# State space stage: outer products through PSUM, recursion by pairs and fours, pads in three pools

## The chip, the cores and the metric
The kernel runs on one core of a Trainium2 chip. The metric is the device time of one launch in microseconds (us), as the median of several runs. Times inside an execution come from one profiled run, in us from the start of its span. The engines are PE (TensorE, the matmuls; PEld are its weight loads), DVE (VectorE), ACT (ScalarE), POOL (GpSimd) and SP, which here only issues DMAs.

## The reference
Two networks in a row on 256 tokens of width 1024, batch 1, all in float32. The first block is a state space (S5) mixer, a squared-ReLU MLP and a gate; the second is two layers of a mixer with four branches and a gated MLP, with shift, scale and gate vectors made from a conditioning vector by `w_ada`. The change lies in the mixer of the first block:

```
ab  = exp(lam * dt)                       # (64 groups, 64 states), complex
bb  = (ab - 1) / lam * b                  # input matrices, 16 channels a group
bu  = einsum('blgh,gph->blgp', u, bb)     # complex
xs[t] = ab * xs[t-1] + bu[t]              # over the 256 tokens
y   = Re(xs @ c) + d * u
out = gated linear unit of gelu(y)
...
mod = silu(c_2) @ w_ada + b_ada           # 6 vectors for each later layer ("ada")
```

## The kernel before, in words
The kernel is built with a scheduler, which lays the instructions of each engine in one fixed order; each engine then runs its own list and waits on semaphores.

The mixer cuts the 256 tokens into 32 chunks of 8. It has five parts.

1. *Parameters.* `s5_params` makes the powers of `ab` (`pr`, `pi` for exponents in a chunk, `pr2`, `pi2` for the output side) by small DVE operations of 128x32.
2. *The b products.* For each of eight group sets `b_outer` (L597 to L602) multiplies `bb` by powers: DVE makes two products (L597, L600), POOL two others (`ta`, L598, `tb`, L601), DVE combines them (L599, L602) into `pt`. PE transposes `pt` (L655), ACT copies it (`pmt`, L656), PE multiplies `u` with it (L660), ACT copies (`ss`, L662), PE transposes again (L666), ACT writes `zb` (L670): the state that each chunk adds.
3. *The scan.* 30 steps over the chunks (L677 to L680), four DVE operations of 128x64 each: two products, two sums. Every step needs the one before. Then four halves are swapped (L686 to L688) so that `zb` can be the weights of the last product.
4. *The c products.* Sixteen calls of `c_outer` make `ca`, the output matrices times powers: a DVE product (L780), a POOL product (L781) and a sum, on DVE in eight calls and on POOL in eight (L782). From `ca` PE makes the kernel inside a chunk (`kt`, L708), ACT copies it (L716), 32 small DMAs lay it out as `mt` (L720, 27 of them in SP's queue, 5 in POOL's).
5. *The outputs.* PE multiplies `u` by `mt` (L739) and, into the same PSUM tiles, `ca` by `zb` (L751); then come transposes (L762), a gelu and the split into a high and a low part (`y`), and the gated linear unit ("glu"), the first of the long matmuls (L363 to L365, three for each product).

Between these, `ada_next` puts steps of the ada product on PE as filling: a step reads a tile `wa` of 512 KB by SP (L916) into one of three buffers and multiplies it in eight matmuls of 128x256 (L918). The steps that are not done in the mixer are done between the matmuls of glu (seven pairs, the second step of a pair split into four pieces between glu's matmuls) and in the MLP (eight single ones).

DVE and the SBUF side of POOL are shared by parts 2 to 4; the order of SP's queue is that of the code (ada reads, then `mt`, then the weights of the next stage).

Of the kernel before, what the change touches and what calls it, by code (L numbers as in the profile page):

```python
# [9 lines left out]
F32 = mybir.dt.float32  # L10
# [3 lines left out]
ALU = mybir.AluOpType  # L14
# [3 lines left out]
P = 128  # L18
# [260 lines left out]
class Net:  # L279
# [19 lines left out]
    def _t(self, pool, tag, shape, dt, s):  # L299
        tag = tag + self.ln  # L300
        pool = self.late.get(tag, pool)
        return pool.tile(list(shape), dt, tag=tag, bufs=BUFS[tag], name=self.nm(s))

    def k4(self, shape, dt=F32, s="k4"):
        return self._t(self.p4, "k4", shape, dt, s)
# [190 lines left out]
    def s5_params(self):  # L496
# [80 lines left out]
                f, g = slice(64 * half, 64 * half + 64), slice(32 * half, 32 * half + 32)  # L577
                self.S.copy(self.bb3[r, g, 0::2], bb[f, ri].unsqueeze(2).to_broadcast([64, 32, 2, 16]))

        arr, aii = (self.q6.tile([P, 2, 32], F32, name=s) for s in ("arr", "aii"))  # L580
        for r in range(2):
            V.tensor_copy(arr[:, r, :], pr[:, :, 0])
        V.tensor_scalar(aii[:, 0, :], pi[:, :, 0], -1.0, None, op0=ALU.mult)
        V.tensor_copy(aii[:, 1, :], pi[:, :, 0])
        self.arr, self.aii = arr, aii

    def b_outer(self, dst, g0, xr, xi):

        V, G = self.V, self.G
        sh = [P, 4, 8, 16]  # L590
        pr = self.pr[:, g0 : g0 + 4, :].unsqueeze(3).to_broadcast(sh)
# [8 lines left out]
        V.tensor_tensor(dst[:, :, 1], xi, pr, op=ALU.mult)  # L600
        G.tensor_tensor(tb, xr, pi, op=ALU.mult)  # L601
        V.tensor_tensor(dst[:, :, 1], dst[:, :, 1], tb, op=ALU.add)  # L602

    def s5(self):
        V, G, S, T, nc = self.V, self.G, self.S, self.T, self.nc
# [36 lines left out]
        V.memset(zb[:, :, :, 0:1], 0.0)  # L642
        bre, bim = self.bb[:, 0], self.bb[:, 1]
        for jp in range(4):
            ss_sb = self.k4([P, 2, 2, 2, 64], F32, "ss")
            for jj in range(2):
                pt = self.q4.tile([P, 4, 2, 8, 16], F32, tag="pt", name=self.nm("pt"))
                self.b_outer(pt, (jp * 2 + jj) * 4, bre, bim)
                self.ada_next(2)
                pmt = self.k4([P, 4, 2, P], F32, "pmt")  # L650
                for g2 in range(2):
                    ps = self.pm([P, 4, P])
                    for i in range(4):
                        g4, ri = g2 * 2 + i // 2, i % 2
# [13 lines left out]
            for jj in range(2):  # L668
                g0 = (jp * 2 + jj) * 4
                S.copy(zb[:, :, g0 : g0 + 4, 1:32], ps[:, jj, :, :, 0:31])  # L670


        for s in range(1, 31):
            prev, nxt = zb[:, :, :, s], zb[:, :, :, s + 1]
            t1 = self.sm([P, 2, 32])
            t2 = self.sm([P, 2, 32])
            V.tensor_tensor(t1, prev, self.arr, op=ALU.mult)  # L677
            V.tensor_tensor(t2, zb[:, ::-1, :, s], self.aii, op=ALU.mult)
            V.tensor_tensor(t1, t1, nxt, op=ALU.add)
            V.tensor_tensor(nxt, t1, t2, op=ALU.add)  # L680
            if s in (23, 30):

                c = slice(0, 24) if s == 23 else slice(24, 32)
                t = self.bb.rearrange("p a (b e) c -> p (a b) (e c)", e=2)
                cp = V.tensor_copy if s == 23 else S.copy
                cp(t[64:128, :, c], zb[0:64, 1, :, c])  # L686
                V.tensor_copy(zb[0:64, 1, :, c], zb[64:128, 0, :, c])
                cp(zb[64:128, 0, :, c], t[64:128, :, c])  # L688
# [12 lines left out]
        for half in range(2):  # L701
# [898 lines left out]
    def run(self):  # L1600
        tc, nc = self.tc, self.nc
        V, S, G = self.V, self.S, self.G
        with ExitStack() as st:
# [8 lines left out]
            self.psm = pool("psm", 3, space=PSUM)  # L1612
            self.psx = pool("psx", space=PSUM)
# [4 lines left out]
            self.late = {}  # L1618
# [4 lines left out]
            with ExitStack() as s5s:  # L1623
# [145 lines left out]
```

## Time and profile before

| | |
|---|---|
| median of 3 runs | 1995.99 us (1995.98 to 1996.63) |
| the profiled execution's own time | 1997.63 us |
| its span | 1995.9 us |
| PE busy | 1906.2 us (96%) |
| DVE busy | 1548.6 us (78%) |
| ACT busy | 927.4 us (46%) |
| POOL busy | 130.9 us (7%) |
| chain that ended last | PE 84%, DVE 11%, issue 2%, DMA 2%, ACT 1% |

The span is the time from the first to the last instruction; the time of the execution is a little longer. In the page's 40 slices of 49.9 us each, PE is busy in tenths `3869999999...`: it is not full in the first three slices, where the mixer stands, and full from the fourth on. DVE has `9974577699...`: full in the first two.

### The profile page before, as it was taken

What the parts mean: (1) busy time and instruction counts of PE and PEld (TensorE: products, weight loads), DVE (VectorE), ACT (ScalarE), POOL (GpSimd) and SP (SyncE); (2) the same over time, 40 slices, a digit from 0 to 9 for tenths busy, and PEclk for the clock granted to TensorE, in tenths of its full rate; (3) what the DMA queues carried; (4) which work ended last, traced back from release to release, by engine and by line L of the source; (5) the groups of instructions that cost most, each with busy time, mean ns of one, the idle gap of its engine ahead of it and who ended that gap; (6) DMA issues with size and microseconds to landing.
All of it is one profiled execution on the core that took longest, in us unless ns stands there. A gap on an engine that the chain in (4) does not pass through costs nothing.

```text
span 1995.9 us, 35545 instructions
## 1 busy us (share of the span) xinstructions
PE 1906.2 (96%) x13842; PEld 1692.7 (85%) x13842; DVE 1548.6 (78%) x3133; ACT 927.4 (46%) x1583; POOL 130.9 (7%) x138
## 2 busy tenths in 40 slices
PE   3869999999999999999999999999999999999998
PEld 1457899998789998789998777787998789999997
DVE  9974577699987789998778576675689997776665
ACT  2443445455654555664553212212555664544443
POOL 6720000000000011000000000000100000010000
PEclk8989999999999999999999999999999999999998
DMA  5657665554345564236555455454455235555663
GB/s 176 187 187 244 224 199 183 180 183 156 106 125 169 182 191 156 88 106 189 181 187 157 126 163 164 152 165 124 141 178 157 74 108 170 180 180 169 183 187 107
DMA packets 103192, 323.45 MB, mean 162 GB/s; under 512 B 16416, under 2 KB 18608, under 8 KB 102640
## 3 DMA queue, kind: packets, MB, share of 16 engines
q1 hardware_dynamic: 102256, 319.53, 51.3%
q8 instruction: 109, 1.79, 0.4%
q0 software_dynamic: 336, 1.44, 0.2%
q14 instruction: 59, 0.48, 0.1%
q10 hardware_dynamic: 432, 0.21, 0.0%
HBM read 317.47 MB, written 1.05 MB: 160 GB/s over the span
## 4 chain that ended last, share of the span: by engine, by line
PE 84%; DVE 11%; issue 2%; DMA 2%; ACT 1%; SPq 0%; DVEq 0%; ACTq 0%
PE pm L363 21%; PE pm L364 21%; PE pm L365 21%; PE pm L1029 2%; PE pm L1031 2%; PE pm L1030 2%; DVE wl L332 2%; PE px L1351 1%; DVE cy L1060 1%; PE px L1300 1%; PE pm L372 1%; PE pm L373 1%; PE px L918 1%; PE pm L374 1%; PE px L1333 1%
## 5 line engine op out<-in xcount | busy, mean ns | idle before, releaser
L331 ACT CAST wh<-ws 128x1024 fp32r<-128x1024 f32 (+3 forms) x556 | 533.1, 961 | 723.7 <-PE pm L364 410.2
L332 DVE TENSOR_TENSOR wl<-ws,wh 128x1024 fp32r<-128x1024 f32 (+3 forms) x556 | 616.5, 1116 | 267.0 <-ACT wh L331 264.5
L363 PE MATMUL pm<-h,wh 128*128 128x256 f32 (+1 forms) x928 | 301.1, 324 | 0.0
L365 PE MATMUL pm<-h,wl 128*128 128x256 f32 (+1 forms) x928 | 299.5, 323 | 0.0
L364 PE MATMUL pm<-h,wh 128*128 128x256 f32 (+1 forms) x928 | 298.9, 322 | 0.0
L363 PE MATMUL pm<-m,wh 128*128 128x256 f32 (+1 forms) x704 | 213.7, 304 | 0.0
L364 PE MATMUL pm<-m,wh 128*128 128x256 f32 (+1 forms) x704 | 213.2, 303 | 0.0
L365 PE MATMUL pm<-m,wl 128*128 128x256 f32 (+1 forms) x704 | 212.6, 302 | 0.0
L363 PEld LDWEIGHTS pm<-h,wh 128*128 128x128 f32 x928 | 176.1, 190 | 20.7 <-ACT wh L331 4.6
L364 PEld LDWEIGHTS pm<-h,wh 128*128 128x128 f32 x928 | 176.2, 190 | 15.9 <-issue 0.8
L365 PEld LDWEIGHTS pm<-h,wl 128*128 128x128 f32 x928 | 175.7, 189 | 14.9
L363 PE MATMUL pm<-hx,wh 128*128 128x256 f32 x640 | 184.0, 288 | 0.0
L364 PE MATMUL pm<-hx,wh 128*128 128x256 f32 x640 | 180.6, 282 | 0.0
L365 PE MATMUL pm<-hx,wl 128*128 128x256 f32 x640 | 180.2, 281 | 0.0
L1060 DVE SCALAR_TENSOR_TENSOR cy<-up,vecs,cy 128x256 f32<-128x256 f32 x360 | 162.6, 485 | 1.4
L363 PEld LDWEIGHTS pm<-m,wh 128*128 128x128 f32 x704 | 134.1, 191 | 8.5 <-ACT wh L331 1.7
L364 PEld LDWEIGHTS pm<-m,wh 128*128 128x128 f32 x704 | 134.2, 191 | 6.6 <-issue 1.7
L952 DVE SCALAR_TENSOR_TENSOR ac<-wa,sc,ac 128x512 f32<-128x512 f32 x168 | 116.9, 747 | 27.6 <-DMA wa<-w_ada 27.6
L365 PEld LDWEIGHTS pm<-m,wl 128*128 128x128 f32 x704 | 134.2, 191 | 4.9
L429 POOL TENSOR_TENSOR ssq<-ssq,sq 128x256 f32<-128x256 f32 x45 | 43.2, 960 | 1429.2 <-ACT sq L423 1427.8
L363 PEld LDWEIGHTS pm<-hx,wh 128*128 128x128 f32 x640 | 121.1, 189 | 2.2 <-issue 2.0
L364 PEld LDWEIGHTS pm<-hx,wh 128*128 128x128 f32 x640 | 121.4, 190 | 0.3
(439 smaller groups left out, 4278.0 us busy)
## 6 DMA issues: line engine op xcount, KB each, us to landing
wa<-w_ada SPq DMA_DIRECT2D x96, 512.0 KB, 4.0
ws<-w_gp SPq DMA_DIRECT2D x96, 512.0 KB, 3.7
ws<-w_f SPq DMA_DIRECT2D x88, 512.0 KB, 4.4
ws<-w_tok SPq DMA_DIRECT2D x76, 512.0 KB, 4.0
ws<-mlp_w SPq DMA_DIRECT2D x64, 512.0 KB, 4.1
ws<-w_gp SPq DMA_DIRECT2D x96, 256.0 KB, 2.7
ws<-w_f2a SPq DMA_DIRECT2D x32, 512.0 KB, 4.4
ws<-w_cin SPq DMA_DIRECT2D x24, 512.0 KB, 4.5
```

Of the source, the lines that this page charges most:

```text
L331: self.S.copy(hi, src)
L332: self.V.tensor_tensor(lo, src, hi.bitcast(F32), op=ALU.subtract)
L363: self.T.matmul(out, h, ah, start=start and i == 0, stop=False)
L364: self.T.matmul(out, h, al, start=False, stop=False)
L365: self.pe_last = self.T.matmul(out, l, ah, start=False, stop=stop and i == n - 1)
L372: self.T.matmul(out, wh, act.hi(k), start=k == 0, stop=False)
L429: (eng or self.G).tensor_tensor(acc, acc, sq, op=ALU.add)
L952: V.scalar_tensor_tensor(acc[:, v], st[:, i], c, acc[:, v], op0=ALU.mult, op1=ALU.add)
L1029: self.T.matmul(ps, hi, a, start=k == 0, stop=False)
L1030: self.T.matmul(ps, lo, a, start=False, stop=False)
L1031: self.pe_last = self.T.matmul(ps, hi, b, start=False, stop=k == KC - 1)
L1060: V.scalar_tensor_tensor(y[:, k], up[:, k, i : i + L], w[:, i : i + 1], y[:, k], op0=ALU.mult, op1=ALU.add)
```

## The change
Five edits, all but the last in the mixer.

- `b_outer` and `c_outer`: the first product of each pair goes into a PSUM tile `tmp` (one bank, used again by every call), and the power it multiplies with is read from a PSUM copy (`prp`, written by ACT at L698, and again as `prp2` at L731). `ta`, `tb`, `pi`, `dst` stay in SBUF. All sums of `c_outer` are now on DVE.
- The scan: `s5_scan` adds pairs (all odd chunks at once, 4 operations of 128x1024), fours (4 of 128x512), then 7 single steps with the fourth power, and goes back down (4 operations of 128x448, 3 of 128x960). The last sum is written straight into the layout of the weights, `zf` (four DVE operations of 64x480, L633, four ACT copies, L632). `s5_params` makes the square and the fourth power of `ab` for it.
- `ada_next(2)` in the eight steps of part 4: two ada steps each where there was one.
- PSUM: in the mixer the pool of `pm` has 2 buffers where it had 3, `pxa` 2 where it had 3, and a pool `pw` holds `tmp` and `prp`; half 1 of the output tiles reuses those two.
- Pads of 96, 64 and 96 bytes a partition in three SBUF pools, so that operands lie otherwise.

```diff
@@ s5_params
-        arr, aii = (self.q6.tile([P, 2, 32], F32, name=s) for s in ("arr", "aii"))
...
+        for j in range(3):
+            arr, aii = (self.q6.tile([P, 2, 32], F32, name=f"{s}{j}") for s in ("arr", "aii"))
+            if j:
+                t, u = q32(), q32()
+                V.tensor_tensor(t, wi, wi, op=ALU.mult)
+                V.tensor_tensor(u, wr, wr, op=ALU.mult)
+                V.scalar_tensor_tensor(aii[:, 1, :], wr, 2.0, wi, op0=ALU.mult, op1=ALU.mult)
+                V.tensor_tensor(arr[:, 0, :], u, t, op=ALU.subtract)
...
+    def s5_step(self, zb, dst, src, level):
...
+        V.tensor_tensor(t1, zb[:, :, src], arr, op=ALU.mult)
+        V.tensor_tensor(t2, zb[:, ::-1, src], aii, op=ALU.mult)
+        V.tensor_tensor(t1, t1, zb[:, :, dst], op=ALU.add)
+        return t1, t2
+
+    def s5_scan(self, zb):
...
+        add(slice(1, 32, 2), slice(0, 32, 2), 0)
+        add(slice(3, 32, 4), slice(1, 32, 4), 1)
+        for c in range(7, 32, 4):
+            add(slice(c, c + 1), slice(c - 4, c - 3), 2)
+        add(slice(5, 32, 4), slice(3, 29, 4), 1)
+        t1, t2 = self.s5_step(zb, slice(2, 32, 2), slice(1, 31, 2), 0)
...
+                S.copy(zf[half][r, :, 1::2], zb[f, ri, 1::2].rearrange("p c g -> p g c"))
+                V.tensor_tensor(zf[half][r, :, 2::2].rearrange("p g c -> p c g"), t1[f, ri], t2[f, ri], op=ALU.add)
@@ b_outer
-        V.tensor_tensor(dst[:, :, 0], xr, pr, op=ALU.mult)
...
-        V.tensor_tensor(dst[:, :, 0], dst[:, :, 0], ta, op=ALU.subtract)
...
+        V.tensor_tensor(tmp, xr, pr, op=ALU.mult)
+        V.tensor_tensor(dst[:, :, 0], tmp, ta, op=ALU.subtract)
+        V.tensor_tensor(tmp, xi, pr, op=ALU.mult)
+        V.tensor_tensor(dst[:, :, 1], tmp, tb, op=ALU.add)
@@ s5
+        self.tmp = self.pw.tile([P, 512], F32, tag="tmp", name="tmp")
+        self.prp = self.pw.tile([P, 32, 8], F32, tag="prp", name="prp")
+        S.copy(self.prp, self.pr)
...
+        self.prp = self.pw.tile([P, 64, 7], F32, tag="prp", name="prp2")
+        S.copy(self.prp, self.pr2)
...
-            self.ada_next()
+            self.ada_next(2)
...
+        zf = self.s5_scan(zb)
@@ c_outer
-        V.tensor_tensor(c[:, :, 0:7], c1[:, g, :].unsqueeze(2).to_broadcast(sh), pr, op=ALU.mult)
...
-        (G if g0 % 8 else V).tensor_tensor(c[:, :, 0:7], c[:, :, 0:7], ta, op=ALU.add)
+        V.tensor_tensor(tmp, c1[:, g, :].unsqueeze(2).to_broadcast(sh), pr, op=ALU.mult)
+        V.tensor_tensor(c[:, :, 0:7], tmp, ta, op=ALU.add)
@@ pools
+                self.psm = pool("psm5", 2, s5s, space=PSUM)
+                self.pw = pool("pw", 1, s5s, space=PSUM)
+                self.psx = pool("psx5", 1, s5s, space=PSUM)
+                self.bufs = dict(BUFS, pxa=2)
...
+            self.p2.tile([P, 24], F32, tag="pad", bufs=1, name="pad2")
...
+            self.ws.tile([P, 16], F32, tag="pad", bufs=1, name="pads")
...
+            self.up.tile([P, 24], F32, tag="pad", bufs=1, name="padu")
```

The scheduler puts the instructions in another order. Three places follow. First PE in the b products, around the sixth of the eight calls. Before (L655 transposes of `pt`, L660 products with `u`, L918 one ada matmul each from the tiles `wa_497` and `wa_543`):

```order
L655 MATMUL pm_600<-ident,pt_578 128x128
L660 MATMUL px_568<-pmt_555,u_47_281 32x128 x2
L918 MATMUL px_290<-wa_497,sc 32x256
L655 MATMUL pm_600<-ident,pt_578 128x128
L918 MATMUL px_290<-wa_497,sc 32x256
L655 MATMUL pm_600<-ident,pt_578 128x128
L660 MATMUL px_568<-pmt_555,u_47_281 32x128 x2
L660 MATMUL px_568<-pmt_555,u_50_288 32x128 x4
L655 MATMUL pm_600<-ident,pt_578 128x128
L918 MATMUL px_290<-wa_497,sc 32x256
```

Each row of the order that reads 32x256 is two matmuls of the trace. Now at the same place (L710, L715, L721 and L960 are the former L655, L660, L666 and L918):

```order
L715 MATMUL px_543<-pmt_530,u_51_305 32x128 x4
L715 MATMUL px_543<-pmt_530,u_54_312 32x128 x4
L721 MATMUL px_553<-ident,ss_464 128x128 x2
L710 MATMUL pm_583<-ident,pt_561 128x128 x2
L721 MATMUL px_553<-ident,ss_464 128x128 x2
L710 MATMUL pm_583<-ident,pt_561 128x128 x2
L710 MATMUL pm_589<-ident,pt_561 128x128 x4
L960 MATMUL px_314<-wa_570,sc 32x256 x3
L960 MATMUL px_314<-wa_576,sc 32x256
```

The ada matmuls, which stood one by one between the transposes, stand here in one piece.

Second, ACT at the end of the b products. Before (`pmt`: copies of the last two calls; `ca`: 64x64 copies of `c_outer`):

```order
L656 COPY pmt_647<-pm_648 128x512
L656 COPY pmt_647<-pm_654 128x512
L662 COPY ss_629<-px_660 128x256
L656 COPY pmt_692<-pm_693 128x512
L779 ACTIVATE ca_908<-s5v 64x4x16 x2
L929 COPY adas_639<-px_290 128x512
L656 COPY pmt_692<-pm_699 128x512
```

Now (`prp_749` is the copy of `pr2`, which every product of `c_outer` on DVE reads):

```order
L711 COPY pmt_674<-pm_675 128x512
L711 COPY pmt_674<-pm_681 128x512
L971 COPY adas_666<-px_314 128x512
L731 COPY prp_749<-pr_41_252 128x448
L717 COPY ss_656<-px_687 128x256
L965 COPY mod_77<-px_668 128x32
L711 COPY pmt_719<-pm_720 128x512
L711 COPY pmt_719<-pm_726 128x512
```

A new copy stands behind the copies of the seventh call's `pmt` and that of an ada result, ahead of those of the eighth call.

Third, DVE among the c products. Before (L780 and L782 the product and the sum of `c_outer`, L677 to L680 one step of the scan):

```order
L780 TENSOR_TENSOR ca_946<-s5v,pr_41_248 128x4x112 x2
L677 TENSOR_TENSOR sm_722<-zb,arr 128x64
L678 TENSOR_TENSOR sm_723<-zb,aii 128x64
L679 TENSOR_TENSOR sm_722<-sm_722,zb 128x64
L782 TENSOR_TENSOR ca_946<-ca_946,ta_947 128x4x112
L680 TENSOR_TENSOR zb<-sm_722,sm_723 128x64
```

Now (L823 and L824 product and sum, L607 to L609 and L619 the first level of the scan):

```order
L824 TENSOR_TENSOR ca_801<-tmp,ta_802 128x4x112
L607 TENSOR_TENSOR t_187_949<-zb,arr_267 128x1024
L823 TENSOR_TENSOR tmp<-s5v,prp_749 128x448
L608 TENSOR_TENSOR t_188_950<-zb,aii_268 128x1024
L824 TENSOR_TENSOR ca_801<-tmp,ta_808 128x4x112
L609 TENSOR_TENSOR t_187_949<-t_187_949,zb 128x1024
L823 TENSOR_TENSOR tmp<-s5v,prp_749 128x448
L619 TENSOR_TENSOR zb<-t_187_949,t_188_950 128x32x32
```

The first level stands between the c products from the sixth of the sixteen calls on, the second level among the last three calls, and everything from the single steps down stands behind the last call but for its first operation.

## Rows read from the trace of the kernel before

**Rows 1.** Windows: stretch, length, busy us of each engine, PE's clock, DMA share.

```profile
50.00:100.00 50.00, 42.12 (x600) 24.18 (x600) 48.19 (x65) 22.81 (x67) 35.33 (x28) 0.91 0.60 186
150.00:200.00 50.00, 50.00 (x348) 37.89 (x349) 21.02 (x30) 19.32 (x31) 3.69 (x5) 1.00 0.72 244
```

**Rows 2.** Timeline, PE: start, us, line, operation, count, idle before and its releaser.

```profile
118.49 1.13 PE L739 MATMUL px<-mt,u 128*32 128x128 f32 x24
...
128.91 4.35 PE L751 MATMUL pm<-ca,zb 128*32 128x128 f32 x96 [9.29 <-ACT zb L688]
...
142.56 0.28 PE L363 MATMUL pm<-y,wh 128*128 128x256 f32 x1
```

**Rows 3.** Timeline, DVE, the scan: first operations of two successive steps.

```profile
125.78 0.26 DVE L677 TENSOR_TENSOR sm<-zb,arr 128x64 f32<-128x64 f32 x1
...
126.71 0.26 DVE L677 TENSOR_TENSOR sm<-zb,arr 128x64 f32<-128x64 f32 x1
```

**Rows 4.** Timeline, POOL: the last c sum, and five of the mt DMAs.

```profile
104.42 1.14 POOL L782 TENSOR_TENSOR ca<-ca,ta 128x448 f32<-128x448 f32 x1 [1.64 <-DVE ca L780]
107.39 3.08 POOL L720 DMA_DIRECT2D mt<-kt  x5 [1.83 <-ACT kt L716]
```

**Rows 5.** Timeline, DVE: last b call, first c call, start of the scan.

```profile
66.59 1.43 DVE L600 TENSOR_TENSOR pt<-bb,pr 128x512 f32<-128x512 f32 x1
67.95 0.68 DVE L599 TENSOR_TENSOR pt<-pt,ta 128x512 f32<-128x512 f32 x1
...
69.15 2.65 DVE L780 TENSOR_TENSOR ca<-s5v,pr 128x448 f32<-128x448 f32 x2
...
79.10 0.96 DVE L677 TENSOR_TENSOR sm<-zb,arr 128x64 f32<-128x64 f32 x1
```

**Rows 6.** Timelines of POOL and DVE, 1041 to 1050 us; px is in PSUM.

```profile
1041.18 2.82 POOL L429 TENSOR_TENSOR ssq<-ssq,sq 128x256 f32<-128x256 f32 x3 [130.54 <-ACT sq L423]
...
1041.62 0.97 DVE L988 SCALAR_TENSOR_TENSOR h<-k,mod,h 128x256 fp32r<-128x256 f32 x1
1042.51 0.86 DVE L986 SCALAR_TENSOR_TENSOR k<-cx,g,px 128x256 f32<-128x256 f32 x2
...
1049.91 0.48 DVE L988 SCALAR_TENSOR_TENSOR h<-k,mod,h 128x256 fp32r<-128x256 f32 x1
```

**Rows 7.** Timeline, PE, first and last of the b products, ada matmuls between them.

```profile
49.11 0.43 PE L660 MATMUL px<-pmt,u 128*32 128x128 f32 x8 [2.26 <-DVE u L634]
...
62.00 0.62 PE L918 MATMUL px<-wa,sc 128*32 128x256 f32 x2
62.55 0.33 PE L655 MATMUL pm<-ident,pt 128*128 128x128 f32 x1
...
77.51 0.44 PE L666 MATMUL px<-ident,ss 128*128 128x128 f32 x2 [0.51 <-ACT ss L662]
```

**Rows 8.** Timeline, ACT: the last writes of zb.

```profile
78.19 0.60 ACT L670 COPY zb<-px 128x248 f32<-128x248 f32 x2
```

**Rows 9.** Lines by form, 0 to 170 us: count, busy us, mean ns of one.

```profile
L332 DVE TENSOR_TENSOR wl<-ws,wh 128x1024 fp32r<-128x1024 f32 x12 | 14.8, 1242 | 13.5 <-ACT wh L331 13.5
L626 DVE TENSOR_REDUCE sm<-sq 128x32 f32<-128x1024 f32 x2 | 3.8, 1916 | 0.2 <-ACT sq L624 0.2
```

**Rows 10.** Timeline, PE in glu (an ada pair, from its start) and MLP (one step).

```profile
148.41 0.64 PE L918 MATMUL px<-wa,sc 128*32 128x256 f32 x8
...
152.66 0.28 PE L365 MATMUL pm<-y,wl 128*128 128x256 f32 x1
...
277.77 0.64 PE L918 MATMUL px<-wa,sc 128*32 128x256 f32 x8 [1.47 <-DMA wa<-w_ada]
```

**Rows 11.** The tile wa, 0 to 160 us: its reads from issue to landing.

```profile
DMA to landing us min/median/max: 3.4/4.2/10.7
```

**Rows 12.** Timeline, SP: the issues of mt.

```profile
91.42 24.19 SPq L720 DMA_DIRECT2D mt<-kt  x27
```

**Rows 13.** Line L332, one tile read from PSUM: ns min/median/max, first and last start.

```profile
L332 DVE TENSOR_TENSOR zf<-pm,zf x6: 680/684/692, 535.2 to 1595.7; 128x512 fp32r<-128x512 f32 x6
```

More of the change, by code (lines that the diff above doesn't have):

```diff
@@ L301, in _t @@
         pool = self.late.get(tag, pool)
-        return pool.tile(list(shape), dt, tag=tag, bufs=BUFS[tag], name=self.nm(s))
+        return pool.tile(list(shape), dt, tag=tag, bufs=self.bufs[tag], name=self.nm(s))
     def k4(self, shape, dt=F32, s="k4"):
@@ L578, in s5_params @@
                 self.S.copy(self.bb3[r, g, 0::2], bb[f, ri].unsqueeze(2).to_broadcast([64, 32, 2, 16]))
-        arr, aii = (self.q6.tile([P, 2, 32], F32, name=s) for s in ("arr", "aii"))
[L581 to L585, printed above, removed]
+        self.am = []
+        wr, wi = pr[:, :, 0], pi[:, :, 0]
@@ new lines, in s5_params @@
+        for j in range(3):
[6 more added lines that the diff above has]
+                V.tensor_tensor(arr[:, 0, :], u, t, op=ALU.subtract)
+            else:
+                V.tensor_copy(arr[:, 0, :], wr)
+                V.tensor_copy(aii[:, 1, :], wi)
+            wr, wi = arr[:, 0, :], aii[:, 1, :]
+            V.tensor_copy(arr[:, 1, :], wr)
+            V.tensor_scalar(aii[:, 0, :], wi, -1.0, None, op0=ALU.mult)
+            self.am.append((arr, aii))
@@ new lines, in s5_step @@
+    def s5_step(self, zb, dst, src, level):
+        V = self.V
+        arr, aii = self.am[level]
+        n = len(range(32)[dst])
+        sh = [P, 2, n, 32]
+        arr, aii = (v.unsqueeze(2).to_broadcast(sh) for v in (arr, aii))
+        new = self.k4 if n > 8 else self.k2 if n > 1 else self.sm
+        t1, t2 = new(sh, F32, "t1"), new(sh, F32, "t2")
+        V.tensor_tensor(t1, zb[:, :, src], arr, op=ALU.mult)
+        V.tensor_tensor(t2, zb[:, ::-1, src], aii, op=ALU.mult)
+        V.tensor_tensor(t1, t1, zb[:, :, dst], op=ALU.add)
+        return t1, t2
@@ new lines, in s5_scan, with add @@
+    def s5_scan(self, zb):
+        V, S = self.V, self.S
+        def add(dst, src, level):
+            t1, t2 = self.s5_step(zb, dst, src, level)
+            V.tensor_tensor(zb[:, :, dst], t1, t2, op=ALU.add)
+        zf = [self.k4([P, 32, 32], F32, "zf") for _ in range(2)]
+        add(slice(1, 32, 2), slice(0, 32, 2), 0)
[4 more added lines that the diff above has]
+        t1, t2 = self.s5_step(zb, slice(2, 32, 2), slice(1, 31, 2), 0)
+        for half in range(2):
+            f = slice(64 * half, 64 * half + 64)
+            for ri in range(2):
+                r = slice(64 * ri, 64 * ri + 64)
+                S.copy(zf[half][r, :, 1::2], zb[f, ri, 1::2].rearrange("p c g -> p g c"))
+                V.tensor_tensor(zf[half][r, :, 2::2].rearrange("p g c -> p c g"), t1[f, ri], t2[f, ri], op=ALU.add)
+            V.memset(zf[half][:, :, 0:1], 0.0)
+        return zf
@@ L590, in b_outer @@
         sh = [P, 4, 8, 16]
-        pr = self.pr[:, g0 : g0 + 4, :].unsqueeze(3).to_broadcast(sh)
+        tmp = self.tmp.rearrange("p (g i h) -> p g i h", g=4, h=16)
+        pr = self.prp[:, g0 : g0 + 4, :].unsqueeze(3).to_broadcast(sh)
         pi = self.pi[:, g0 : g0 + 4, :].unsqueeze(3).to_broadcast(sh)
@@ L641, in s5 @@
         zb = self.q6.tile([P, 2, 32, 32], F32, name="zb")
-        V.memset(zb[:, :, :, 0:1], 0.0)
+        V.memset(zb[:, :, 0:1, :], 0.0)
         bre, bim = self.bb[:, 0], self.bb[:, 1]
+        self.tmp = self.pw.tile([P, 512], F32, tag="tmp", name="tmp")
+        self.prp = self.pw.tile([P, 32, 8], F32, tag="prp", name="prp")
+        S.copy(self.prp, self.pr)
         for jp in range(4):
@@ L669, in s5 @@
                 g0 = (jp * 2 + jj) * 4
[L670 to L688, printed above, removed]
+                S.copy(zb[:, :, 1:32, g0 : g0 + 4].rearrange("p r c g -> p r g c"), ps[:, jj, :, :, 0:31])
         ca = {}
         c1, c2 = (par(s).rearrange("p (g h) -> p g h", h=16) for s in ("c1", "c2"))
+        self.prp = self.pw.tile([P, 64, 7], F32, tag="prp", name="prp2")
+        S.copy(self.prp, self.pr2)
         for j in range(8):
@@ L733, in s5 @@
             for jq in range(2):
-                with self.lane("a"):
-                    ps = pss[half, jq] = self.px([P, 4, 8, 16]) if half and jq else self.pm([P, 4, 8, 16])
+                ps = pss[half, jq] = (self.pw.tile([P, 4, 8, 16], F32, tag=("prp", "tmp")[jq], name=self.nm("py"))
+                                      if half else self.pm([P, 4, 8, 16]))
                 for j4 in range(4):
@@ L750, in s5 @@
                             g = j * 4 + g4
-                            T.matmul(ps[32 * g4 : 32 * g4 + 32, j4].rearrange("p s h -> p (s h)"), zb[:, half, g, :],
+                            T.matmul(ps[32 * g4 : 32 * g4 + 32, j4].rearrange("p s h -> p (s h)"), zf[half][:, g, :],
                                      ca[half * 4 + g // 8][:, g % 8].rearrange("p s h -> p (s h)"), start=False, stop=j4 == 3)
@@ L772, in c_outer @@
         g = slice(g0, g0 + 4)
-        pr = self.pr2[:, g].unsqueeze(3).to_broadcast(sh)
+        pr = self.prp[:, g].unsqueeze(3).to_broadcast(sh)
         pi = self.pi2[:, g].unsqueeze(3).to_broadcast(sh)
@@ L779, in c_outer @@
             self.S.activation(c[r, :, 7, :], c1[r, g, :], AF.Copy, scale=1.0 - 2.0 * ri)
-        V.tensor_tensor(c[:, :, 0:7], c1[:, g, :].unsqueeze(2).to_broadcast(sh), pr, op=ALU.mult)
+        tmp = self.tmp[:, 0:448].rearrange("p (g i h) -> p g i h", g=4, h=16)
         G.tensor_tensor(ta, c2[:, g, :].unsqueeze(2).to_broadcast(sh), pi, op=ALU.mult)
-        (G if g0 % 8 else V).tensor_tensor(c[:, :, 0:7], c[:, :, 0:7], ta, op=ALU.add)
+        V.tensor_tensor(tmp, c1[:, g, :].unsqueeze(2).to_broadcast(sh), pr, op=ALU.mult)
+        V.tensor_tensor(c[:, :, 0:7], tmp, ta, op=ALU.add)
     def ple_proj(self):
@@ L1610, in run @@
             self.p2 = pool("p2")
+            self.p2.tile([P, 24], F32, tag="pad", bufs=1, name="pad2")
             self.p4 = pool("p4")
-            self.psm = pool("psm", 3, space=PSUM)
-            self.psx = pool("psx", space=PSUM)
             self.vecs = self.c.tile([P, NVEC], F32, name="vecs")
@@ L1617, in run @@
             self.x = self.c.tile([P, KC, L], F32, name="x")
-            self.late = {}
+            self.late, self.bufs = {}, BUFS
             self.ones = self.c.tile([P, P], F32, name="ones")
@@ L1646, in run @@
                 nc.scalar.dma_start(self.rope.rearrange("p a b c -> p (a b c)"), self.a["rope"])
+            self.psm = pool("psm", 3, space=PSUM)
+            self.psx = pool("psx", space=PSUM)
+            self.bufs = BUFS
             self.stage, self.ada_off = self.k4, 0
             self.ws = pool("ws", 3)
+            self.ws.tile([P, 16], F32, tag="pad", bufs=1, name="pads")
             self.wr = pool("wr", 4)
             self.up = pool("up", 1)
+            self.up.tile([P, 24], F32, tag="pad", bufs=1, name="padu")
             self.ph = pool("ph", NH)
```

2 lines of the change are left out of this document (removed).

## The prediction, made before the changed kernel was run
> **What bounds the kernel now.** I read the windows first, then the ends of the mixer on PE, then DVE's and POOL's timelines inside it. [...] The scan's steps come 0.93 us apart at its end [rows 3]; the last c sum ends on POOL at 104.42 + 1.14 = 105.56 [rows 4], so 23.35 us pass from the last `ca` to L751. The c products themselves run from 69.15 to 105.56, 36.4 us, with the scan's first steps among them.
>
> DVE and POOL slow each other. The b product beside POOL came 1.36 us before its successor (66.59 to 67.95); the two sums behind it, with POOL waiting, took 1.20 together [rows 5]. Two rows late in the kernel tell what a PSUM operand does: with POOL busy from 1041.18 to 1044.00, the operation on SBUF alone took 0.97 us, against 0.48 with POOL idle, and the two that read `px` in PSUM took 0.86 together [rows 6], as two without a neighbour would. The change gives every outer product and sum of DVE one operand or result in PSUM.
>
> **The change part by part.** *Start of the b products.* Twelve small DVE operations (128x32) for the powers: four of 128x64 take 0.93 [rows 3], so 12 x 0.19 = +2.3 us on the first product with `u` (49.11 to 51.4). The b products themselves fall from 1.36 to about 0.72 (0.68 and a wait for the predecessor, since all four now pass through one `tmp`), so DVE ends long before PE.
>
> *zb.* PE needs 28.8 us from its first `u` product to the last transposes (49.11 to 77.95) [rows 7]. Between them the ada matmuls lie in 21 pieces in the trace; by the new order in 13. A piece of two between single transposes costs 0.55 (62.00 to 62.55) [rows 7], a whole step of eight hardly more (0.64 [rows 10]), so I count pieces: -8 x 0.55 = -4.4. The pool with 2 `pm` buffers instead of 3 could cost up to a PSUM copy's 0.6 for each of 8 calls, 5 us, or nothing; PE has other matmuls to do meanwhile, and I leave it at nothing. So the last transposes end at 51.4 + 24.4 = 75.8 and `zb` at 77.0 (before: 78.19 + 0.60 = 78.8 [rows 8]).
>
> *Start of the c products.* Every L823 reads `prp2`, and ACT writes it behind the seventh call's `pmt`, which PE sets. Eight calls share 24.4 us, 3.05 each; 1.8 calls before the end of `zb` is 71.5. Behind the waiting L823 stand, on DVE, all c products and the scan, and POOL's products stop once their `ta` buffers are full. DVE is idle before that: this costs 2.35 against 69.15.
>
> *c products and first levels.* 32 DVE operations of 128x448 by 0.655 (0.68 for 512 elements less 0.06, and 0.03 for the chain through `tmp`) = 21.0 us, where 8 of them came in 9.95 us (69.15 to 79.10 [rows 5]). The eight sums that POOL did are in this. Level 0: four operations of 1024 elements, 1.24 long [rows 9] and 1.15 apart, 4.6; level 1: four of 512, 0.60 apart, 2.4. These lie in SBUF, beside POOL's 16 products. Free of them it is +0; if all stood beside POOL at 1.36/0.60 they cost 7.0 x 1.27 = +9. POOL was busy 35 of 50 us [rows 1]; without a third of its c operations and ahead of DVE, I put it beside a third of them: +3. The sum is 31.0, against 36.4: the last `ca` at 102.5, 3.1 earlier.
>
> *Tail.* Before, from the last `ca` to L751, 23.35. Now two branches run from 102.5. The scan: 7 steps by 0.93 = 6.4 (a part of the first stands before), four of 448 elements 2.6, three of 960 by 1.15 = 3.4, memsets 0.3, and two of the four strided writes into `zf`, after which half 0 can start. A write of 64x480 is not in the trace: 0.65 if it goes as a contiguous one, and 0.98 by the strided read of L626 (1.916 for 1024 elements against 1.24, so +0.66 ns an element [rows 9]); I take 0.9, as the nearest row is strided: 1.8. With 0.5 for ACT and PE that is 15.0. The other branch is `kt`, the `mt` DMAs and L739: before, 105.56 to 118.49 + 1.13 = 119.62 [rows 2], 14.1, and some 1.5 where `mt` queues behind the ada reads. Either puts L792 (L751 before) at about 117.5, 11.4 earlier than 128.91.
>
> [...]
>
> *From L792 to glu.* 142.56 - 128.91 = 13.65 [rows 2]. The 24 products of the gate's projection that filled PE between the transposes now stand behind them; +0.9.
>
> *Ada moved.* By the order the eight single steps of the MLP go into the mixer, where PE waits anyway, and one more pair is put into glu (eight pairs now, seven before). A single step is eight matmuls in 0.57 (0.64 less the overlap), 4.6 in all, and one waits 1.47 for its tile [rows 10]: 6.0 gone. The pair takes 148.41 to 152.66, 4.25, with five glu matmuls of 0.12 among them [rows 10]: 3.7 back. -2.3; bounds -6.0 (the pair hidden) and +2 (the singles in gaps that stay).
>
> *Price nothing.* The pads change addresses only: DVE has 29 of 50 us free where PE is full [rows 1]. PSUM operands at the DVE: by `zf<-pm`, 0.684 against 0.68 [rows 13, 5], no charge for a read; a write into PSUM has no row, bounds 0 and, if it ran as slowly as a contended one, the last rival below.
>
> [...]
>
> **Sum.** -11.4 + 0.9 - 2.3 = -12.8 us. It is made on the span, 1995.9; the profiled execution took 1997.63, 1.73 more, and the median 1995.99. The same difference on the median gives 1983 us. With the bounds of zf (-0.5, +0.2), contention (-3, +6), `pm` buffers (+5) and ada (-3.7, +4.6), not all at once: 1978 to 1989.
>
> **The rivals.**
> - *PE is not the limit of the b products* (20%). If L710 comes as fast as DVE delivers, `prp2` is ready at 66, `zb` at 71.5, and all behind them 5.5 earlier; with the `zf` writes at their lower bound, 1977. For it: eight b products cost 8 x 2.9 = 23 us on DVE from about 43. Against: PE was 42 of 50 busy there [rows 1].
> - *The end hangs on transfers* (13%). SP's queue has 32 ada reads ahead of the 27 `mt` copies, where it had 26, and each read waits until PE has left one of three buffers. If the last goes some 7 us late, the second branch ends at about 124 and half the gain is gone: 1990. For it: the reads take 3.4 to 10.7 us [rows 11], and `mt` stood 24.19 us in the queue [rows 12]. Against: at the median of 4.2 three buffers give a tile in 1.4 us, and 11 tiles in 77 to 102.5 need one in 2.3.
> - *The same place, slower than before* (5%). At a landing of 10.7 a tile comes in 3.6 us; 11 tiles from 77 end at 116. Behind them 27 issues by 0.62 (five took 3.08 [rows 4]) and 4.0 to the end of L739: 136.7, 19 late, 2002. It decides from the point where the last read goes at 110, that is a landing of 9.0.
> - *PSUM takes nothing off the contention* (7%), because both products still read a second operand from SBUF. Then the 32 operations stay at 9.95/8 = 1.24: 32 x 0.585 = +18.7, 2002. For it: the writes into PSUM have no row. Against: rows 6.
>
> **How the numbers follow.** The forecast has 55%, the rivals 20, 13, 5 and 7. The range 1973 to 1993 leaves out the two slow cases (12%) and the ends of the others. Within 0.2% of 1995.99, which is what a measurement of this kernel can just tell from no change (4 us), lie the edge of the transfer case and parts of the slow ones: 6%. Slower by more: 8%. Faster: 86%.
>
> **What would show it.** DVE L650 and L652 at 0.7 with POOL busy beside them (1.4: the last rival). ACT's `prp2` copy at 71 (66: the first). The last `ca` at 102, the first operation of L792 at 117.5 and what it waits for: ACT or DVE `zf` (forecast), L780 still busy behind a DMA of `mt` (transfers). The first L363 on `y` at 132. Wrong it is above all if PE's wait before L792 is longer than 4 us, or if the gain of the mixer comes back as waits of the glu matmuls for their weights, which are read in the same queue.

## The result: 1973.5 us, and the profile after

| | median us | runs | ratio to before |
|---|---|---|---|
| before, beside the changed kernel | 1996.31 | 1995.98 to 1999.2 | |
| changed | 1973.52 | 1969.56 to 1979.86 | 0.9882 [0.9866, 0.9898] |

The change gains 1.2%, some 23 us, where 13 were forecast. The profiled execution took 1979.86 us (span 1978.1), the longest of the four. Its rows are compared with those of before stage by stage, and for the sum the medians count. Part of what that execution lost can be seen: the mean granted clock of PE is 0.74 of full speed in one stretch of it where before has 1.00 (changed, then before):

```profile
1420.00:1440.00 20.00, 18.41 (x104) 17.14 (x103) 11.97 (x33) 7.87 (x13) 2.17 (x2) 0.74 0.37 113
```

```profile
1420.00:1440.00 20.00, 19.92 (x162) 18.74 (x161) 16.09 (x43) 10.37 (x21) 4.49 (x5) 1.00 0.54 156
```

Over the whole span the mean granted clock was 0.987 in this execution and 0.990 to 0.991 in the other three.

First the mixer. DVE, timeline of the changed kernel (start, us, line, operation; L823 and L824 are the former L780 and L782, L607 to L619 the scan, L633 the `zf` writes), and with it POOL:

```profile
69.74 0.63 DVE L823 TENSOR_TENSOR tmp<-s5v,prp 128x448 f32<-128x448 f32 x1 [3.74 <-ACT prp L731]
70.47 0.62 DVE L824 TENSOR_TENSOR ca<-tmp,ta 128x448 f32<-128x448 f32 x1
71.13 0.63 DVE L823 TENSOR_TENSOR tmp<-s5v,prp 128x448 f32<-128x448 f32 x1
...
78.24 1.44 DVE L608 TENSOR_TENSOR t<-zb,aii 128x1024 f32<-128x1024 f32 x1
...
97.41 0.62 DVE L824 TENSOR_TENSOR ca<-tmp,ta 128x448 f32<-128x448 f32 x1
...
108.86 3.92 DVE L633 TENSOR_TENSOR zf<-t,t 64x480 f32<-64x480 f32 x4
```

```profile
71.18 0.94 POOL L822 TENSOR_TENSOR ta<-s5v,pi 128x448 f32<-128x448 f32 x1 [4.15 <-DVE ca L824]
...
76.81 1.79 POOL L822 TENSOR_TENSOR ta<-s5v,pi 128x448 f32<-128x448 f32 x1 [0.51 <-ACT ca L820]
```

The product at 71.13 runs in 0.63 us beside POOL's at 71.18, as the one at 69.74 does with POOL idle; POOL's takes 0.94, and the one before it, at 66.08 with DVE idle, 0.95: here neither slows the other. In before two DVE products took 2.65 together [rows 5], and the two of POOL beside them 2.61:

```profile
68.70 2.61 POOL L781 TENSOR_TENSOR ta<-s5v,pi 128x448 f32<-128x448 f32 x2 [1.23 <-DVE pt L599]
```

The scan's operation at 78.24 has all operands in SBUF and takes 1.44, against 1.24 for 1024 elements in before [rows 9], and POOL beside it 1.79. The last `ca` ends at 98.03 (105.56 before [rows 4]), and the last `zf` write at 112.8.

PE, timeline of the changed kernel; the bracket is the idle time before it and what ended that (L960 is ada, L780 the products with `mt`, L792 those with `zf`):

```profile
92.71 0.64 PE L960 MATMUL px<-wa,sc 128*32 128x256 f32 x8 [2.57 <-DMA wa<-w_ada]
...
101.08 0.64 PE L960 MATMUL px<-wa,sc 128*32 128x256 f32 x8 [1.67 <-DMA wa<-w_ada]
...
112.63 4.05 PE L780 MATMUL pm<-mt,u 128*32 128x128 f32 x56 [2.37 <-DMA mt<-kt]
116.26 2.94 PE L780 MATMUL py<-mt,u 128*32 128x128 f32 x60
118.96 0.30 PE L792 MATMUL pm<-ca,zf 128*32 128x128 f32 x2
...
135.61 0.28 PE L363 MATMUL pm<-y,wh 128*128 128x256 f32 x1
```

The chain of waits of the changed kernel, in order of time (start, us, engine or transfer):

```profile
80.88 4.89 DMA wa<-w_ada
...
86.52 6.15 DMA wa<-w_ada
...
97.11 6.53 DMA mt<-kt
...
115.51 0.61 SPq L761
...
117.79 7.20 DMA ws<-w_glu
```

PE no longer waits for the scan: `zf` is ready 6 us before L792. PE stands still for ada tiles among the `kt` products (2.57 and 1.67 us above), then for `mt` (2.37), whose DMAs SP issues one by one, most of them some 0.65 apart, and the weights of glu come behind them in that queue. Glu starts at 135.61, 7.0 earlier than before [rows 2]; the forecast had 132.

Then the rest. The same 50 us in the MLP of the first block, before and after; the first bracketed count is PE's matmuls:

```profile
300.00:350.00 50.00, 50.00 (x419) 49.93 (x418) 38.71 (x56) 26.21 (x35) 0.00 (x0) 1.00 0.58 180
```

```profile
300.00:350.00 50.00, 49.88 (x440) 49.68 (x439) 36.98 (x46) 24.78 (x31) 0.00 (x0) 1.00 0.64 196
```

PE is full and at its full clock (1.00) in both, and yet it does 440 matmuls where it did 419. Lines by form from 300 to 400 us (mean ns of one), before and after:

```profile
L363 PE MATMUL pm<-h,wh 128*128 128x256 f32 x128 | 36.2, 283 | 0.0
```

```profile
L363 PE MATMUL pm<-h,wh 128*128 128x256 f32 x128 | 35.3, 276 | 0.0
```

The *pitch*, the time from the start of one matmul to the start of the next, shows it more directly. Four in a row, before and after:

```profile
330.19 0.28 PE L365 MATMUL pm<-h,wl 128*128 128x256 f32 x1
330.31 0.28 PE L363 MATMUL pm<-h,wh 128*128 128x256 f32 x1
330.43 0.28 PE L364 MATMUL pm<-h,wh 128*128 128x256 f32 x1
330.55 0.28 PE L365 MATMUL pm<-h,wl 128*128 128x256 f32 x1
```

```profile
310.07 0.28 PE L365 MATMUL pm<-h,wl 128*128 128x256 f32 x1
310.18 0.28 PE L363 MATMUL pm<-h,wh 128*128 128x256 f32 x1
310.29 0.28 PE L364 MATMUL pm<-h,wh 128*128 128x256 f32 x1
310.41 0.28 PE L365 MATMUL pm<-h,wl 128*128 128x256 f32 x1
```

In this block of before, two back-to-back matmuls of 256 columns start 120 ns apart; in the changed kernel 113 or 118. The forecast does not have this part of the gain.

### The profile page after: what moved, and what is told of

It reads as the page before. It is cut to its first block, busy times and chain, and to the rows that moved or that the text cites. A ratio compares the mean times of both kernels' runs of the same rounds, so it can differ in the third digit from the quotient of the medians.

```text
span 1978.1 us, 35512 instructions
## 1 busy us (share of the span) xinstructions
PE 1890.7 (96%) x13842; PEld 1676.3 (85%) x13842; DVE 1525.5 (77%) x3078; ACT 932.4 (47%) x1587; POOL 112.1 (6%) x130
## 3 DMA queue, kind: packets, MB, share of 16 engines
q8 instruction: 109, 1.79, 0.4%
q0 software_dynamic: 336, 1.44, 0.2%
## 4 chain that ended last, share of the span: by engine, by line
PE 79%; DVE 12%; DMA 4%; ACT 2%; issue 2%; SPq 1%; POOL 0%; DVEq 0%; ACTq 0%; POOLq 0%
PE pm L363 19%; PE pm L364 19%; PE pm L365 18%; DVE wl L332 4%; PE pm L1071 3%; PE pm L1072 3%; PE pm L1073 3%; DVE cy L1102 2%; DMA wa<-w_ada 2%; PE px L960 2%; PE px L1393 2%; PE px L1342 1%; PE px L1375 1%; PE px L404 1%; ACT wh L331 1%
## 5 line engine op out<-in xcount | busy, mean ns | idle before, releaser
L332 DVE TENSOR_TENSOR wl<-ws,wh 128x1024 fp32r<-128x1024 f32 (+3 forms) x556 | 616.1, 1116 | 270.7 <-ACT wh L331 267.7
L363 PE MATMUL pm<-h,wh 128*128 128x256 f32 (+1 forms) x928 | 297.8, 321 | 0.0
L365 PE MATMUL pm<-h,wl 128*128 128x256 f32 (+1 forms) x928 | 296.8, 320 | 0.0
L363 PE MATMUL pm<-m,wh 128*128 128x256 f32 (+1 forms) x704 | 211.6, 301 | 0.0
L365 PE MATMUL pm<-m,wl 128*128 128x256 f32 (+1 forms) x704 | 210.6, 300 | 0.0
L363 PEld LDWEIGHTS pm<-h,wh 128*128 128x128 f32 x928 | 174.6, 188 | 18.5 <-ACT wh L331 4.2
L365 PEld LDWEIGHTS pm<-h,wl 128*128 128x128 f32 x928 | 174.6, 188 | 14.4
L363 PE MATMUL pm<-hx,wh 128*128 128x256 f32 x640 | 183.3, 286 | 0.0
L365 PE MATMUL pm<-hx,wl 128*128 128x256 f32 x640 | 179.6, 281 | 0.0
L363 PEld LDWEIGHTS pm<-m,wh 128*128 128x128 f32 x704 | 132.2, 188 | 9.3 <-ACT wh L331 1.7
L994 DVE SCALAR_TENSOR_TENSOR ac<-wa,sc,ac 128x512 f32<-128x512 f32 x168 | 117.8, 749 | 28.8 <-DMA wa<-w_ada 28.8
L365 PEld LDWEIGHTS pm<-m,wl 128*128 128x128 f32 x704 | 132.5, 188 | 5.7
L363 PEld LDWEIGHTS pm<-hx,wh 128*128 128x128 f32 x640 | 121.0, 189 | 2.2 <-issue 2.0
L365 PEld LDWEIGHTS pm<-hx,wl 128*128 128x128 f32 x640 | 121.0, 189 | 0.0
```

The costliest lines, as they stand in the source:

```text
L332: self.V.tensor_tensor(lo, src, hi.bitcast(F32), op=ALU.subtract)
L363: self.T.matmul(out, h, ah, start=start and i == 0, stop=False)
L365: self.pe_last = self.T.matmul(out, l, ah, start=False, stop=stop and i == n - 1)
L994: V.scalar_tensor_tensor(acc[:, v], st[:, i], c, acc[:, v], op0=ALU.mult, op1=ALU.add)
```

## The experiments

All times are medians; ratios are to executions of the kernel before taken beside them. Two theories for the missing 10 us. *P*: the pads change PE's pitch. *M*: the mixer gave all of it.

**pads_only.** Before with the pads.

```diff
+            self.p2.tile([P, 24], F32, tag="pad", bufs=1, name="pad2")
+            self.ws.tile([P, 16], F32, tag="pad", bufs=1, name="pads")
+            self.up.tile([P, 24], F32, tag="pad", bufs=1, name="padu")
```

> The kernel before with the three pads and nothing else. Theory P: the pads set the moving operand of the long f32r matmuls and the weights that PE loads beside it 64 bytes apart modulo 128, where they lay 0 apart; PE's pitch of back-to-back 128x256 matmuls falls from 120 ns to 113 or 118, and this is the part of the gain that the forecast missed: 6 to 12 us faster than before (1984 to 1990). Rival M: the pads do nothing, the whole gain comes from the mixer: within 3 us of before, pitch 120.

1980.37 us, 0.9910 [0.9897, 0.9923]: 18 us faster with not one instruction added or moved. P in direction; its size was set at half. Window 300 to 350 of this kernel:

```profile
300.00:350.00 50.00, 50.00 (x427) 49.85 (x427) 38.63 (x54) 26.39 (x34) 0.00 (x0) 1.00 0.59 188
```

**no_pads.** The changed kernel with those three lines taken out.

> The changed kernel without its three pads. Theory P: the mixer alone gives what the forecast said of it, 9 to 13 us, so 1983 to 1987, with the pitch back at 120 ns. Rival M: 1971 to 1976, as with the pads.

1993.01 us, 0.9969 [0.9959, 0.9979]. M falls: the mixer and the ada steps together give 5 to 6 us, and 0.9969 x 0.9910 = 0.9879 is the whole change. But the mixer gives less than the forecast too. Its PE timeline:

```profile
101.75 1.08 PE L960 MATMUL px<-wa,sc 128*32 128x256 f32 x8 [4.39 <-DMA wa<-w_ada]
...
116.42 4.29 PE L780 MATMUL py<-mt,u 128*32 128x128 f32 x60 [2.60 <-DMA mt<-kt]
...
135.86 0.28 PE L363 MATMUL pm<-y,wh 128*128 128x256 f32 x1
```

**no_pads_serial.** As no_pads with the scan of before (L677 to L688) in the place of `s5_scan`.

> As no_pads, with the 30 serial steps in place of pairs and fours. If the mixer's end hangs on the mt transfers (first L792 at 119.0 in the changed kernel, with L780 busy up to 119.3 behind waits for mt): the scan ends at about 120 to 123 and the time is 1 to 6 us over no_pads. If it hangs on the scan, as the forecast's first branch has it: 8 to 12 us over no_pads.

1991.40 us, 0.9962 [0.9950, 0.9974]: not slower than no_pads, where 1 to 6 us more were expected. Glu starts at 137.94 instead of 135.86, so pairs and fours are worth 2 us at the end of the mixer, and they do not show in the total. PE waits for the scan again, but only from 121.5 on:

```profile
123.62 3.40 PE L809 MATMUL pm<-ca,zb 128*32 128x128 f32 x64 [2.16 <-ACT zb L743]
```

In the two profiles the 2 us are still there at 940 us, and by 970 no_pads is behind by as much. It waits longer for DVE near 951 (3.00 us against 1.34), and its PE is then granted less than the full clock (0.50 of it from 950.2 to 957.0). Window 940 to 970 of no_pads, of no_pads_serial and of ada1 (below):

```profile
940.00:970.00 30.00, 27.00 (x204) 26.62 (x204) 23.03 (x58) 13.70 (x25) 0.00 (x0) 0.89 0.54 165
```

```profile
940.00:970.00 30.00, 28.66 (x241) 28.40 (x240) 26.10 (x66) 16.23 (x30) 0.00 (x0) 1.00 0.57 185
```

```profile
940.00:970.00 30.00, 27.89 (x222) 27.64 (x221) 25.36 (x67) 16.35 (x31) 0.00 (x0) 0.94 0.56 173
```

So a total that differs by 2 us does not measure the scan. Whether the other executions of the two kernels lose time at this place is not known.

**no_pads_sbuf.** As no_pads, outer products in SBUF: `c_outer` as shown, `b_outer` in the same way, and without the two copies `prp`.

```diff
-        V.tensor_tensor(tmp, c1[:, g, :].unsqueeze(2).to_broadcast(sh), pr, op=ALU.mult)
-        V.tensor_tensor(c[:, :, 0:7], tmp, ta, op=ALU.add)
+        V.tensor_tensor(c[:, :, 0:7], c1[:, g, :].unsqueeze(2).to_broadcast(sh), pr, op=ALU.mult)
+        V.tensor_tensor(c[:, :, 0:7], c[:, :, 0:7], ta, op=ALU.add)
```

> As no_pads, with the outer products back in SBUF (no tmp, no prp; all sums of c_outer stay on DVE). Forecast: beside POOL the products come at 1.2 to 1.4 us again where they came at 0.7; the 16 c products cost 8 to 12 us more, the last ca comes as much later, and the time is 6 to 12 us over no_pads. Rival: the scan made the gain and the PSUM operands none: within 3 us of no_pads.

1999.91 us, 1.0011 [1.0000, 1.0021]: 7 to 8 over no_pads, and no faster than before. The time is as expected, the place is not: the last `ca` comes at 100.9 instead of 97.5, 3 us later and not 8 to 12, and most of the DVE time shows in the scan, with `zf` complete at 123.3 instead of 112.4. The groups of DVE's c operations, 0 to 130 us, here and in the changed kernel:

```profile
L816 DVE TENSOR_TENSOR ca<-s5v,pr 128x448 f32<-128x448 f32 x16 | 19.7, 1269 | 0.0
L817 DVE TENSOR_TENSOR ca<-ca,ta 128x448 f32<-128x448 f32 x16 | 9.2, 612 | 0.0
```

```profile
L823 DVE TENSOR_TENSOR tmp<-s5v,prp 128x448 f32<-128x448 f32 x16 | 10.0, 626 | 4.1 <-ACT prp L731 3.7
L824 DVE TENSOR_TENSOR ca<-tmp,ta 128x448 f32<-128x448 f32 x16 | 10.0, 622 | 1.1
```

With one operand and the result in PSUM the product takes half (0.63 us against 1.27). The sum takes 0.61 on SBUF alone and 0.62 from PSUM; in both kernels POOL's next product waits for it (L817 ended 6.6 us of POOL's idle time, L824 11.1).

**ada1.** As no_pads with one ada step.

```diff
-            self.ada_next(2)
+            self.ada_next()
```

> As no_pads, with one ada step in each of the eight steps of the c products, as before. Theory T (the mixer's end hangs on the mt transfers, because PE, in its fixed order, stands still for ada tiles between the kt products: 0.8 to 4.4 us seven times in no_pads, so that the last kt copy comes at 107.5, 9 us after the last ca): the waits for tiles go, the last kt copy comes at 99 to 103 and the first L363 on y 2 to 6 us earlier than in no_pads; the eight steps come back between the later matmuls at some 5 us, so the time is within 3 us of no_pads. Rival S (the scan is what PE waits for): the first L363 on y does not move, and the time is 4 to 6 us over no_pads.

1983.27 us, 0.9935 [0.9921, 0.9949], 7 us under no_pads by the ratios and 10 by the medians, where within 3 us was expected. The mixer does what theory T says, last `kt` copy at 100.4 and glu 5.3 earlier. What T has come back did so in small part. Of the two profiles, no_pads loses 4.1 us in glu (first L363 on `y` to first on `h`), where it has an eighth ada pair, and wins 5.3 from there to the end of the MLP, where the single steps are gone. After 400 us it loses 4.8 again, some 2 of them in the window 940 to 970 shown above; the rest is not placed. Its PE timeline:

```profile
111.44 3.81 PE L780 MATMUL py<-mt,u 128*32 128x128 f32 x60 [3.07 <-DMA mt<-kt]
...
130.55 0.28 PE L363 MATMUL pm<-y,wh 128*128 128x256 f32 x1
```

**ada1_serial.** As ada1 with the scan of before.

> As ada1 (no pads, one step), with the 30 serial steps of the scan. In ada1 L780 ends at 115.3 and zf is complete at 113.8, so the scan is no longer far behind the transfers. If pairs and fours matter once the transfers are early: the serial scan ends at 120 to 123 as in no_pads_serial, the first L363 on y comes 4 to 7 us later than the 130.55 of ada1, and the time is 3 to 7 us over ada1's 1983.3. If they do not: within 2 us of ada1.

1994.17 us, 0.9980 [0.9971, 0.9989]: by the ratios 9 us over ada1, and by the medians 11. With the ada waits gone the scan is what ends last: pairs and fours are worth 7.5 us at glu's start (138.06 against 130.55), where they were worth 2 beside two steps. PE, this kernel:

```profile
122.72 3.64 PE L809 MATMUL pm<-ca,zb 128*32 128x128 f32 x64 [4.04 <-ACT zb L743]
...
138.06 0.28 PE L363 MATMUL pm<-y,wh 128*128 128x256 f32 x1
```

**ada1_sbuf.** As ada1 with the edit of no_pads_sbuf.

> As ada1 (no pads, one step), with the outer products back in SBUF and all sums of c_outer on DVE. With the ada waits out of the way the contention with POOL shows in full: 8 to 14 us over ada1's 1983.3, the last ca at 106 to 110. If the ada waits hid nothing of it: 7 us over, as no_pads_sbuf over no_pads.

1991.11 us, 0.9962 [0.9949, 0.9976]: 5 us over ada1 by the ratios, 8 by the medians. That is what was expected if the ada waits hid nothing of it. The last `ca` came at 100.7, not at 106 to 110; the delay shows in the scan, as in no_pads_sbuf (`zf` complete at 123.3, against 113.8 in ada1).

**The pads, three other sizes**, each on the kernel before: `pad_all96` keeps the first pad only (96 bytes), the others have one pad in pool `ws`, of 32 and of 128 bytes.

> The kernel before with the first pad only (96 bytes), which moves the moving operands (pool p4) and the weights (pool wr) by the same 96 bytes, so that they stay 0 apart modulo 128. If the distance counts: pitch 120, within 2 us of before. If the place itself counts (32 modulo 256 for the moving operand, as in the changed kernel): 8 to 18 us faster.

> The kernel before with a pad of 32 bytes in pool ws only: weights and moving operands of the first block 32 apart modulo 128, those of hc and hx too, as they were before. If the distance counts, the 120 ns of the first block fall to the mixture of 116, 118 and 122 that hx has at this distance, mean 118.3, and the time falls by some 6 us (about 4000 pairs x 1.5 ns). If only a distance of 64 helps: within 2 us of before.

> The kernel before with a pad of 128 bytes in pool ws only. If the pattern repeats every 128 bytes: pitch 120 and within 2 us of before. If it repeats every 256 or more, the distance is now the farthest: pitch 113 to 118, 8 to 18 us faster.

1996.68 us, 0.9999 [0.9988, 1.0009]; 1998.16, 1.0008 [0.9998, 1.0018]; 1994.14, 0.9982 [0.9973, 0.9991]. Here the distance counts and not the place: moving both by 96 leaves 120 ns. With the pad of 32 the first block gets the pitch that hx always had at this distance, as expected, but not the 6 us: in the MLP 370 successive matmuls of 512 columns on `m` went from 227 to 233 ns, which takes 2 back, and the rest of the miss is open. With the pad of 128 neither expectation holds: the pitch is 118.5 instead of 119.3 and the gain 4 us, so the pattern does not repeat at 128.

**pads_ada1** (the changed kernel with one ada step) and **pads_ph** (the same, and the third pad 128 bytes larger, so that hc and hx lie at the same place modulo 256 as the others).

```diff
-            self.up.tile([P, 24], F32, tag="pad", bufs=1, name="padu")
+            self.up.tile([P, 56], F32, tag="pad", bufs=1, name="padu")
```

> The changed kernel with one ada step in each of the eight steps of the c products, as before: pads and one step together. If the two gains are independent (the pads act on the pitch behind the mixer, the step on waits in the mixer): -0.9% and -0.65% add up, 1997.5 x 0.991 x 0.9935 = 1967, 4 to 9 us under the changed kernel. If they share a cause: 1971 to 1976, as the changed kernel. Pitch: 113 and 118 again, in stretches of some tens of us that need not be those of the other padded profiles.

> As pads_ada1, with the third pad 128 bytes larger: hc and hx (pool ph) move from 160 to 32 modulo 256, where the other moving operands lie, so that they are 64 below the weights and not 64 above. If the place modulo 256 decides whether the pitch of 113 can hold: hx and hc get stretches at 113 as h and m have, their mean of 117.8 falls to about 116, and 2800 pairs of 256 columns give 4 to 6 us: 1962 to 1968. If only the distance modulo 128 counts: 117.8 as before and within 3 us of pads_ada1's 1971.4.

1971.42 us, 0.9863 [0.9845, 0.9881], and 1965.57, 0.9831 [0.9816, 0.9845]. By the ratio pads_ada1 lies between its two expectations, and by the median at the edge of the second: 0.9845 was expected of independent gains, and only the end of the interval reaches it. Its interval overlaps that of the changed kernel (0.9882 [0.9866, 0.9898]), so with the pads in place the second ada step is not shown to cost anything in the total, though with one step glu starts 3.9 us earlier (131.72). pads_ph beats both kernels of the case, 0.5% below the changed one; 0.3% of this goes with the larger pad, the intervals of pads_ada1 and pads_ph just touching. Lines by form, 590 to 690 us, of before, of the changed kernel and of pads_ph:

```profile
L363 PE MATMUL pm<-hc,wh 128*128 128x256 f32 x176 | 50.6, 287 | 0.0
```

```profile
L363 PE MATMUL pm<-hc,wh 128*128 128x256 f32 x179 | 50.8, 284 | 0.0
```

```profile
L363 PE MATMUL pm<-hc,wh 128*128 128x256 f32 x176 | 49.4, 281 | 0.0
```

The pitch in one table, from the starts of successive matmuls of L363 to L365 with 256 columns (pairs under 135 ns apart). The distance is the moving operand's byte address in its partition less that of the weights, as the programs were laid out, modulo 256:

| kernel | distance, others | mean ns | at 115 or less | distance, hc and hx | mean ns | at 115 or less |
|---|---|---|---|---|---|---|
| before | 0 | 119.3 | 1% | 224 | 118.3 | 4% |
| pad_w32 | 224 | 118.3 | 4% | 224 | 118.3 | 4% |
| pad_w128 | 128 | 118.5 | 17% | 224 | 118.2 | 5% |
| changed | 192 | 116.1 | 40% | 64 | 117.8 | 1% |
| pads_only | 192 | 115.9 | 43% | 64 | 117.8 | 1% |
| pads_ph | 192 | 114.0 | 86% | 192 | 114.2 | 81% |

Some 5,200 pairs stand in the first class and 2,700 in the second. From before to pads_only the mean falls by 2.34 ns, which on 7,900 pairs is 18.5 us, about what pads_only gains. The first class is not of one kind. In before, 3,000 pairs of it have 119.9. The 1,130 on the `z` operands of the second block have 118.9, though they lie at distance 0 too. The 1,000 of the last MLP have 117.8, with two thirds of them on the part of `h` that lies in another pool, at 224. Nor is the distance all that counts: from pads_ada1 to pads_ph the `z` operands and their weights stay where they are, and their pitch falls from 117.2 to 114.2.

## Why the prediction was wrong

*The step that failed is "Price nothing: the pads change addresses only".* It bounded the pads by what DVE could gain, and DVE was free. PE's busy share of 50.00 in 50 [rows 1] was read as PE at its peak; it says only that PE was never idle: before did 419 matmuls in 50.00 us from 300 on, pads_only 427. The pitch was to be seen in the timeline of before: 120 ns for 256 columns in the first block, and 116 to 122 for hx in the same kernel at another address. pads_only, with no other edit, gives 17.6 us by the medians.

*The mixer's sum, -11.4, was right about DVE and wrong about what ends last.* DVE's side was early: `ca` at 98.0 instead of 102.5. The first product with `u` came at 48.0 and not 51.4 (the twelve small operations did not delay it), contention with POOL cost 0.4 us in the first level (two operations of 1.44, two of 1.22) and not 3, and the start of L823 at 69.74 hung on `prp2`, as forecast (71.5). Of the smaller prices, a c operation came 0.70 us after the other (0.655), and a `zf` write took 0.96 (0.9). The sum L824, which reads `tmp` in PSUM, takes 0.622 us where the same sum on SBUF alone, L817 of no_pads_sbuf, takes 0.612.

But L792 started at 118.96 and glu at 135.61 (forecast 117.5 and 132), behind the waits for `mt`. That is the rival on transfers, held at 13%, in kind; in size it was less, for it had the second branch end at about 124. The forecast put 1.5 us on `mt` behind the ada reads and nothing on PE, which in its fixed order waits for tiles among the `kt` products (2.57 and 1.67 us for the last two). ada1 shows the price without the pads: with one ada step glu starts 12.0 us earlier than before, where the forecast's mixer has 10.5, and the time is 13 lower (0.9935), 7 to 10 us under no_pads. Of this 5.3 us stand at glu's start; the part that came up after 400 us is not explained by the mixer.

*From L792 to glu*, +0.9 was forecast and 16.65 - 13.65 = +3.0 measured. The chain of waits goes through the weights of glu (117.79 to 124.99), which stand behind `mt` in SP's queue; no run tests that alone.

*Ada moved*, -2.3: from the profile of before to that of no_pads +3.3 in glu and -5.5 from there to the end of the MLP, -2.2 in all.

The two errors had opposite signs, a gain of 18 us missed and a loss not seen (7 to 10 us without the pads, some 4 with them and these within the noise). That the time still came out at the edge of the range, 1973.5 by the median and 1972.4 by the ratio (0.9882 of 1995.99) against 1973, is luck. *PSUM takes nothing off the contention* and the two other rivals fell.

## What to carry to other kernels

A full PE at its full clock is not yet PE at its peak (419 and 427 matmuls in the same 50.00 us here): divide a stretch by its matmuls, and compare the pitch between groups of the same shape in one trace; where it differs, operand addresses are a candidate, and a pad of some tens of bytes is a cheap experiment (of the pads tried alone, three sizes gave 0.2% or less). An edit that fills waiting time with transfers (the second ada step) must be read in the queue and in PE's order, where it can become the wait; and the worth of an edit (pairs and fours: 2 or 7.5 us at glu's start) depends on which of two chains ends last. Read such a worth first at the end of the stage: in no_pads a wait of 3.00 us and a granted clock of 0.50 near 951 us, far behind it, took back the 2 us.

## What the runs showed of the hardware that was not expected

- The pitch of the back-to-back 128x256 matmuls of L363 to L365 goes with the distance of moving operand and weights: 120 ns at 0 (but a mean of 118.9 for `z`), 116 to 122 at 224, 113 or 118 at 192. At 192 either value holds for stretches of tens of us (113 from 280 to 400 us, 118 from 240 to 280 in the changed kernel); pads_ph, where all operands lie alike, has 113 in most. What picks the value, and why a distance of 64 has hardly anything but 117 to 119, is open. The spread of the changed kernel's executions (1969.56 to 1979.86) may come of it or of the clock shown above; neither was tested.
- The distance that suits 256 columns need not suit 512: with the three pads the 512-column matmuls on `m` went from 227 to 233 ns (distance 0 to 192), while those on `h`, of which a third went from 0 to 192 and two thirds from 224 to 64, fell from 232.5 to 230.4.
- In the changed kernel the DVE sum L824, which reads the PSUM result of the product before it, starts 0.73 us after that product's start, 0.10 after its end (69.74, 0.63, then 70.47); the next product follows its sum at 0.66 (71.13).
